# Layer two's input projections as seven block products in place of eight (Strassen's scheme)

## The chip, the cores and the metric

The kernel runs on one core of one Trainium2 chip. A core has five engines with an instruction stream each: PE (TensorE, matrix products into PSUM), DVE (VectorE), ACT (ScalarE), POOL (GpSimd) and SP (SyncE, which here issues nearly all DMAs). They work side by side and wait for each other by semaphores; 16 DMA engines move data between DRAM and the on-chip memory, SBUF. PE adds products up in PSUM, eight banks of 128 partitions x 512 fp32 values; DVE and ACT read PSUM, POOL cannot.

The metric is the device time of one execution in microseconds (us), as a median of several.

## The reference, cut to what matters

Two layers over 1024 tokens (a grid of 16 rows x 64 columns) and 256 context tokens, 1024 features. Layer one is attention with grouped keys; layer two, where the change is, attends within a window of 8 x 16 grid places and to the context:

```python
hx = rms_norm(x, norm_g[i]) * (1.0 + sc_x) + sh_x          # x: 1024 tokens x 1024 features
hc = rms_norm(ctx, norm_g[i]) * (1.0 + sc_c) + sh_c        # ctx: 256 tokens
px = hx @ w_in                                             # w_in: 1024 x 4096, columns q | k | v | z
pkv = hc @ w_in[:, B_WIDTH:3 * B_WIDTH]                    # the context's k and v
...                                                        # attention of 16 heads of 64, with a bias by position
yx = (o * jax.nn.silu(z)) @ w_out
x = x + g_x * yx
return rms_norm(x, final_norm_g)
```

The product `hx @ w_in`, 1024 x 1024 by 1024 x 4096, is the one that is changed.

## The kernel before, in words

**Precision.** PE multiplies fp16 numbers. Each fp32 operand is split into a high and a low fp16 part, and each product is three matmuls: high x high, high x low, low x high, added up in PSUM. Weights are scaled by WS = 32 before they are split. So every operand that reaches PE costs a cast (high) and a subtraction (low) first.

**Tiles.** Tokens come in eight tiles of 128 (t = 0 to 7) and two of context (8, 9). Features are eight chunks of 128 (KT = 8). Heads go in pairs, u = 0 to 7: a pair has 128 columns each of q, k, v and z (the gate).

**Layer two, pair by pair.** `b_load(u)` (L1339) loads the pair's weights, eight blocks of 128 x 512, through a staging tile; `load_w` (L664) splits them with one ACT cast (L670) and one DVE operation (L671) per block. `b_qk(u)` (L1347, matmuls L1360) projects q and k with the weights as stationary operand and 512 tokens as moving one, 24 matmuls to a bank; `b_vz(u)` (L1382, L1393 and, for the context, L1396) projects v and z with a token tile as stationary operand and the 256 weight columns of v and z as moving one. Both use the two PSUM banks called pj in turn, and DVE and ACT take each finished bank out: L1374 to L1379 for q and k, L1403 to L1409 for v and the gate. `b_att(u)` (L1412) computes scores (L1424, L1425), adds the bias on DVE (L1444), takes maxima (L1451), exponentiates on ACT (L1462 to L1465), splits the probabilities (L1042 on DVE or L1045 on POOL), transposes them by DMA, multiplies by v (L1473, L1475) and scales the output (L1491). `o_out` (L1055) splits and transposes it into the tile `ob`. Two tiles of ob are of tag Y0 and the rest of tag Y1.

**The order.** Generators yield after each piece of work, and `timeline` (L478) merges them by written virtual times: pair u's attention from u to u + 1, beside it the projections of pair u + 1 (`b_proj`, L1503) and, from u + 0.5, the weight load of pair u + 2. A `Planner` (L47) then sets the final order on each engine: it simulates the program with a cost for each instruction, works out by when each result is due, and reorders by that. In it, POOL's additions and DVE's operations on two SBUF operands shut each other out (`lock`, L148). Pair 0's projections run before any attention of layer two.

**From layer one to layer two.** `a_out(t)` (L1254, matmuls L1275) projects layer one's output for a token tile in two halves of 512 columns, 24 matmuls each; DVE multiplies by the gate vector (L1279) and POOL adds the residual (L1280). `b_ln(t)` normalises the tile through `ln_tile` (L642): a sum of squares on ACT, the reciprocal root on POOL, two DVE passes on each half, an ACT cast and a DVE subtraction, and two DMA transposes (L661) into `hb_hi` and `hb_lo`, which hold all ten tiles for the whole of layer two. L1516 writes the order: tile t's normalisation beside the output projection of later tiles.

```python
    run_all(steps("l0 o4 l1 o5 l2 o6 l3 o7 l4 o80 l5 o90 l6"))
```

Here `l` is `b_ln` of a tile, `o` is `a_out` of a tile (with a second digit, one half of it).

**The end.** `load_wout` (L1215) brings the output weights, in two sets of tiles (tags X0, X1) that the pairs' weights used before: the first half from virtual time 6.05 on, the second from 7.0 on. `b_out(t, tag)` (L1547, matmuls L1566) does the output projection, the residual, the final norm and the store.

## Time and profile before

| | |
|---|---|
| runs | 1361.56 us median of 3 (1360.18 to 1363.06) |
| profiled execution | 1365.58 us, its span 1363.8 us |
| PE busy | 1329.9 us, 13183 matmuls |
| DVE, ACT, POOL busy | 1003.1, 910.2, 664.7 us |
| one pair of layer two (917.76 to 979.85) | 62.09 us: PE 61.98, DVE 45.55, ACT 45.65, POOL 15.77 busy |

The profile is of one execution. Its page gives the busy time of each engine and, in 40 equal slices of the span, each engine's busy share in tenths and the clock granted to PE. The chain of waits is the chain of work that ended last, followed back from the last instruction; each row has a start, a length and what ran or was waited for. The stretches give the busy time of each engine between two moments. The groups list instructions by source line, engine and operands, with a count, busy time, the mean ns of one, and the idle time in front of them with what ended it. In operand names the numbers are left out: `pb<-hb_hi,wb` is a matmul into a bank `pb...`. A line can be a helper's.

### The profile page before, as it was taken

To read this page: it belongs to the slowest core of one execution; us is meant where nothing else is said; L and a number is where in the kernel's file an instruction comes from. 1 tells how busy PE (TensorE), PEld (TensorE's weight loads), DVE (VectorE), ACT (ScalarE), POOL (GpSimd) and SP (SyncE) were. 2 spreads that over 40 slices of the span, in tenths; PEclk is the share of its full clock that TensorE was granted. 3 is DMA by queue.
4 is the path that set the end of the run, shared out by engine and by line. 5 is a ranking of instruction groups with operands and counts; after the bars stand their busy time and mean duration, and the time that the engine had idled before them with its cause. 6 is when DMAs were issued, how large, how long until landed. Compare 5 with 4: busy or idle time off the path is not lost.

```text
span 1363.8 us, 34709 instructions
## 1 busy us (share of the span) xinstructions
PE 1329.9 (98%) x13183; PEld 927.6 (68%) x13183; DVE 1003.1 (74%) x2647; ACT 910.2 (67%) x2186; POOL 664.7 (49%) x855
## 2 busy tenths in 40 slices
PE   9999999999999999999999999999999999999897
PEld 6457777777777777776554486777768686867543
DVE  5788788878788789887276846777776867777743
ACT  3653788888787876878632437777776777786711
POOL 2573787777778775788743201312222222332332
PEclk9999999999999999999999999999999999999999
DMA  9652577878789777847066725666576656677932
GB/s 352 186 162 76 108 145 156 154 161 166 149 152 169 146 150 138 172 145 210 10 171 175 178 80 120 125 132 138 117 153 110 156 96 146 113 159 141 194 101 102
DMA packets 426959, 198.23 MB, mean 145 GB/s; under 512 B 382560, under 2 KB 389664, under 8 KB 426792
## 3 DMA queue, kind: packets, MB, share of 16 engines
q1 hardware_dynamic: 426216, 195.98, 65.3%
q8 instruction: 103, 1.69, 0.5%
q14 instruction: 64, 0.52, 0.1%
q10 hardware_dynamic: 576, 0.03, 0.0%
HBM read 90.51 MB, written 15.22 MB: 78 GB/s over the span
## 4 chain that ended last, share of the span: by engine, by line
PE 68%; DVE 11%; ACT 9%; DMA 5%; POOL 3%; issue 3%; SPq 1%; DVEq 0%; POOLq 0%; ACTq 0%
PE pa L946 11%; PE pb L1360 9%; PE pvz L1393 9%; PE poa L1275 7%; PE pob L1566 6%; PE st L1183 2%; PE st L1184 2%; PE pkv L817 2%; ACT bpf L1464 2%; PE pm L976 2%; PE bpv L1473 1%; PE pv L1052 1%; PE qpv L1104 1%; PE pv L1053 1%; PE pv L1051 1%
## 5 line engine op out<-in xcount | busy, mean ns | idle before, releaser
L1045 POOL TENSOR_TENSOR pl<-pf,ph 128x256 f16<-128x256 f32 x340 | 234.1, 714 | 58.2 <-ACT pf L1170 44.5
L1045 POOL TENSOR_TENSOR bph<-bpf,bph 128x256 f16<-128x256 f32 (+1 forms) x128 | 99.9, 790 | 319.5 <-ACT bpf L1464 256.3
L946 PE MATMUL pa<-wa,x 128*128 128x256 f16 x1536 | 213.4, 272 | 0.1
L1360 PE MATMUL pb<-hb_hi,wb 128*128 128x512 f16 (+1 forms) x640 | 193.3, 358 | 1.4 <-DVE bk L1379 1.0
L1393 PE MATMUL pvz<-wb,hb_hi 128*128 128x256 f16 x1024 | 175.4, 273 | 0.6 <-DVE bk L1379 0.3
L946 PEld LDWEIGHTS <-x 128*128 128x128 f16 x1536 | 143.2, 97 | 35.7 <-issue 1.3
L1168 ACT ACTIVATE ph<-st 128x512 f16<-128x512 f32 x200 | 119.1, 604 | 60.7 <-PE st L1184 50.0
L1360 PEld LDWEIGHTS <-wb 128*128 128x128 f16 x960 | 92.7, 98 | 72.5 <-issue 2.9
L1393 PE MATMUL pvz<-wb,hb_lo 128*128 128x256 f16 x512 | 139.6, 273 | 0.0
L1170 ACT ACTIVATE pf<-st 128x512 f32<-128x512 f32 x200 | 119.3, 609 | 1.7 <-POOL pl L1045 1.6
L977 DVE TENSOR_REDUCE mxp<-pm 128x1 f32<-128x512 f32 x160 | 107.9, 684 | 13.7 <-PE pm L976 12.3
L1045 POOL TENSOR_TENSOR qpp<-qpf,qpp 128x512 f16<-128x512 f32 x84 | 97.9, 1186 | 38.4 <-ACT qpf L1127 32.2
L1360 PE MATMUL pb<-hb_lo,wb 128*128 128x512 f16 (+1 forms) x320 | 114.4, 358 | 0.0
L1393 PEld LDWEIGHTS <-hb_hi 128*128 128x128 f16 x1024 | 97.1, 98 | 24.2 <-DVE bk L1379 1.1
L1051 PE MATMUL pv<-v,ph 128*128 128x65 f16 x800 | 104.0, 193 | 0.2 <-ACT ph L1168 0.2
L1052 PE MATMUL pv<-v,ph 128*128 128x64 f16 x800 | 104.0, 195 | 0.0
L1053 PE MATMUL pv<-v,pl 128*128 128x65 f16 x800 | 101.4, 192 | 0.5 <-POOL pl L1045 0.5
L1566 PE MATMUL pob<-wob,ob 128*128 128x512 f16 x384 | 86.7, 379 | 2.6 <-DVE bmx L1444 0.9
L1051 PEld LDWEIGHTS <-ph 128*128 128x128 f16 x800 | 75.8, 97 | 19.0 <-ACT ph L1168 0.7
L1462 ACT ACTIVATE bph<-bpf,bnx 128x384 f16<-128x384 f32 (+1 forms) x128 | 68.7, 582 | 27.2 <-DVE bnx L1454 27.1
L1052 PEld LDWEIGHTS <-ph 128*128 128x128 f16 x800 | 75.5, 97 | 12.6
L1053 PEld LDWEIGHTS <-pl 128*128 128x128 f16 x800 | 76.1, 99 | 10.5 <-POOL pl L1045 1.6
(272 smaller groups left out, 3812.1 us busy)
## 6 DMA issues: line engine op xcount, KB each, us to landing
wg<-in_w_mod SPq DMA_DIRECT2D x64, 256.0 KB
wsb<-in_b_in SPq DMA_DIRECT2D x64, 256.0 KB
wm<-in_w_mod SPq DMA_DIRECT2D x16, 512.0 KB
wsa<-in_a_qz SPq DMA_DIRECT2D x32, 256.0 KB
xstage<-in_x SPq DMA_DIRECT2D x8, 512.0 KB
wsoa<-in_a_w_out SPq DMA_DIRECT2D x16, 256.0 KB
x<-in_x SPq DMA_DIRECT2D x8, 512.0 KB
x_d<-x SPq DMA_DIRECT2D x8, 512.0 KB
```

The lines of the kernel that those rows point to most:

```text
L946: T.matmul(ps[:, :, i, :], hA(a, kt, t), wt[w][:, kt, :], start=n == 0, stop=n == 3 * KT - 1)
L977: V.tensor_reduce(mxs[i][:, t, ch:ch + 1], pm, axis=AX.X, op=ALU.max)
L1045: G.tensor_tensor(lo[:, c], p32[:, c], hi[:, c], op=ALU.subtract)
L1051: T.matmul(pv[:, t, :], hi[:, c], v[:, 0:65], start=first and t == 0, stop=False)
L1052: T.matmul(pv[:, t, 0:HD], hi[:, c], v[:, 65:129], start=False, stop=False)
L1053: T.matmul(pv[:, t, :], lo[:, c], v[:, 0:65], start=False, stop=last and t == n - 1)
L1168: S.activation(ph, st, AF.Exp)
L1170: S.activation(p32, st, AF.Exp)
L1275: T.matmul(ps, lhs(a, kt), w[b][:, kt, :], start=n == 0, stop=n == 3 * KT - 1)
L1360: T.matmul(ps[:, 0:n].rearrange("p (t q) -> p t q", q=P), wt[a][:, kt, which * P:(which + 1) * P], hb[b][:, c0 // P:(c0 + n) // P, kt], st ...
L1393: T.matmul(ps[:, :, j, :], hb[a][:, t, kt], wt[w][:, kt, 256:512], start=m == 0, stop=m == 3 * KT - 1)
L1566: T.matmul(ps, ob[kt][:, t // 4, a, c], wout["b"][hf][b][:, kt, :], start=n == 0, stop=n == 3 * KT - 1)
```

## The change

The product is cut into two halves each way: token tiles 0 to 3 and 4 to 7 (A1., A2.), features 0 to 511 and 512 to 1023, and, among a pair's columns, k against q in one group (g = 0) and v against z in the other (g = 1). A 2 x 2 block product has eight block products; the scheme used (Strassen's, in Winograd's form) has seven, of sums of blocks:

- **Token side.** Stored for the whole layer: A11 and A12 (`top`, tiles 0 to 3), S3 = A11 - A21 and S1 = A21 + A22 (`s31`), S2 = S1 - A11 and S4 = A12 - S2 (`s24`), and A22 (`a22`). `b_ln` of tiles 4 to 7 makes them, on DVE, from the tile and the tile four before it; `b_s24` and `b_a22` split, cast and transpose the rest. The context tiles get a tile of their own. `s24`, `a22` and the context lie in the X tags, which layer one's output weights hold until then.
- **Weight side.** `b_load(u, g)` loads four blocks of 128 x 512 for each group. DVE scales the block; ACT and DVE split three of its four sub-blocks as they are; four sums (in fp32) are made, cast and split on POOL (for pair 0 on DVE and ACT). A block has 7 x 128 columns in each part, where it had 4 x 128.
- **Products.** `b_grp` runs products 1, 2, 6, 5, 7, 3, 4, each of 12 matmuls of 512 columns (g = 0) or 48 of 128 columns (g = 1). Products 1, 6, 7, 4 add up in one bank, 5 and 3 in another, 2 in a third allocation. Between them ACT copies the running sum out to SBUF (`keep`, three times a group) and DVE adds a bank to such a copy (three times a group). q, k, v and z are then taken from these sums in SBUF, and the last from PSUM. `cx` does the context's k or v with as many matmuls as before.
- **Memory.** Layer two's outputs `ob` of pairs 0 to 5 go to DRAM (`ob_d`) and return at virtual time 7.18 into the tiles of `top` and `s31`; all of `ob` is of tag Y0. The output weights become 16 tiles, four of which can be loaded before the last pair's projections end; the others take the place of `s24` and `a22`. The transposed probabilities have 7 buffers for 8.
- **Layer one's end.** `a_out` multiplies in place in PSUM and adds the residual on DVE; tiles 4 to 9 have two buffers for the residual stream. The written order becomes the one in the diff.
- **Planner.** DMA costs go by bytes, and fp16 transfers count half.

```diff
-PFB, PHB, PTB = 5, 5, 8
+PFB, PHB, PTB = 5, 5, 7
...
-            d[u] = y_tile((P, 2, 2, 512), F16, f"{kind}{u}", int(kind == "ob" and u > 1))
+            d[u] = y_tile((P, 2, 2, 512), F16, f"{kind}{u}", 0)
...
-            tm = op.tile([P, 512], F32, name=f"tm{t}{hf}", tag="tm", bufs=2)
-            V.tensor_tensor(tm, ps, gts["t"][:, hc], op=ALU.mult)
-            G.tensor_tensor(x1[:, hc], x1[:, hc], tm, op=ALU.add)
+            V.tensor_tensor(ps, ps, gts["t"][:, hc], op=ALU.mult)
+            V.tensor_tensor(x1[:, hc], ps, x1[:, hc], op=ALU.add)
...
+        if t < 4 or t >= NX:
+            for a, r in enumerate(halves(xt, D, nm)):
+                DM.dma_start_transpose(top[a][:, t] if t < NX else late["cx"][:, t - NX, a], r)
+        else:
+            lo, hi = slice(0, 512), slice(512, D)
+            x0, r = x1s[t - 4], lnp.tile([P, 2, 512], F16, name=f"a22r{t}", tag="a22r", bufs=4)
+            a22r[t - 4] = r
+            S.copy(r[:, 0], xt[:, hi])
+            V.tensor_tensor(r[:, 1], xt[:, hi], r[:, 0], op=ALU.subtract)
+            V.tensor_tensor(xt[:, hi], xt[:, lo], xt[:, hi], op=ALU.add)
+            V.tensor_tensor(xt[:, lo], x0[:, lo], xt[:, lo], op=ALU.subtract)
+            V.tensor_tensor(x0[:, lo], xt[:, hi], x0[:, lo], op=ALU.subtract)
+            V.tensor_tensor(x0[:, hi], x0[:, hi], x0[:, lo], op=ALU.subtract)
+            for a, r in enumerate(halves(xt, D, nm)):
+                DM.dma_start_transpose(s31[a][:, t - 4], r)
...
+    def b_load(u, g):
...
+            DM.dma_start(st.rearrange("p a b -> p (a b)"), b_in[u, g, kt])
+            V.tensor_scalar_mul(st, st, WS)
+            w = bq.tile([P, 2, 7, P], F16, name=f"w{nm}", tag="wb", bufs=8)
+            S.copy(w[:, 0, 0:3], st[:, 0:3])
+            V.tensor_tensor(w[:, 1, 0:3], st[:, 0:3], w[:, 0, 0:3], op=ALU.subtract)
+            ts = bq.tile([P, 4, P], F32, name=f"ts{nm}", tag="ts", bufs=2)
+            E = G if u else V
+            E.tensor_tensor(ts[:, 0], st[:, 3], st[:, 0], op=ALU.subtract)
+            E.tensor_tensor(ts[:, 2], st[:, 2], st[:, 3], op=ALU.subtract)
+            E.tensor_tensor(ts[:, 1], st[:, 2], ts[:, 0], op=ALU.subtract)
+            E.tensor_tensor(ts[:, 3], st[:, 1], ts[:, 1], op=ALU.subtract)
+            if u:
+                G.tensor_copy(w[:, 0, 3:7], ts)
+            else:
+                S.copy(w[:, 0, 3:7], ts)
+            E.tensor_tensor(w[:, 1, 3:7], ts, w[:, 0, 3:7], op=ALU.subtract)
...
+        x_ = bank("x")
+        yield from prod(x_, 1, True)
+        e1 = keep(x_, 1)
+        z_ = bank("z")
+        yield from prod(z_, 2, True)
+        V.tensor_tensor(e1, z_, e1, op=ALU.add)
+        done(0, 0, e1)
+        yield from prod(x_, 6, False)
+        e2 = keep(x_, 2)
+        y_ = bank("y")
+        yield from prod(y_, 5, True)
+        e5 = keep(y_, 5)
+        yield from prod(x_, 7, False)
+        V.tensor_tensor(e5, x_, e5, op=ALU.add)
+        done(1, 4, e5)
+        yield from prod(y_, 3, False)
+        V.tensor_tensor(e2, y_, e2, op=ALU.add)
+        done(1, 0, e2)
+        yield from prod(x_, 4, False)
+        done(0, 4, x_)
+        yield from cx(w)
...
+                        if hf == 1 and u in BSPILL:
+                            DM.dma_start(ob_d[u], ob[u].rearrange("p a b c -> p (a b c)"))
...
-    run_all(steps("l0 o4 l1 o5 l2 o6 l3 o7 l4 o80 l5 o90 l6"))
-    items = [(steps("o81 o91 l7 l8 l9"), 0, 0.8, 5120 * 3 + 450 * 6), (b_load(0), 0.05, 0.6, 8),
-             (b_qk(0), 0.85, 1.8, 23040)]
+    for g in range(2):
+        run_all(b_load(0, g))
+    run_all(steps("l0 l1 o4 l2 o5 l3 l4 o6 l5 o7 l6 o80 l7 o90 x0"))
+    run_all(steps("o81 o91 x1"))
+    side[0] = bq
+    items = [(steps("s0 s1 s2 s3 a0 a1 a2 a3 l8 l9"), 0, 0.1, 3400), (b_qk(0), 0.1, 1.0, C_G)]
...
+            items.append((b_qk(u + 1), u, u + 0.48, C_G))
+            items.append((b_vz(u + 1), u + 0.49, u + 0.97 + 0.2 * l_, C_G))
...
+    items.append((load_wob(0, range(0, 4)), 6.5, 6.9, 4))
+    for j in range(3):
+        items.append((once(lambda j=j: ob_back(j)), 7.18 + 0.001 * j, 7.2, 1))
+    items.append((load_wob(0, range(4, 8)), 7.19, 7.21, 4))
+    items.append((load_wob(1, range(0, 8)), 7.2, 7.3, 8))
```

More of the change, by code (lines that the diff above doesn't have):

```diff
@@ L1297, in trunk_kernel, with x_tiles @@
     bpool = ctx.enter_context(tc.tile_pool(name="bpool", bufs=1))
[L1298 to L1299 removed]
+    top = [bpool.tile([P, 4, KT, P], F16, name=f"top{a}", tag=f"top{a}") for a in range(2)]
+    s31 = [bpool.tile([P, 4, KT, P], F16, name=f"s31{a}", tag=f"s31{a}") for a in range(2)]
+    late = {}
+    def x_tiles(j, nm, shape):
+        return [main.tile(list(shape), F16, name=f"{nm}{a}", tag=f"X{j}{a}") for a in range(2)]
     tc.swap_default_side()
@@ L1303, in trunk_kernel, with halves @@
     tc.swap_default_side()
-    def b_ln(t):
-        yield from ln_tile(lnp, x1s[t], 0 if t < NX else 1, hb_hi[:, t], hb_lo[:, t], f"b{t}")
+    def halves(src, w, nm):
+        r = [lnp.tile([P, D], F16, name=f"r{a}{nm}", tag=f"r{a}", bufs=3) for a in range(2)]
+        for hf in range(w // 512):
+            c = slice(hf * 512, hf * 512 + 512)
+            S.copy(r[0][:, c], src[:, c])
+            V.tensor_tensor(r[1][:, c], src[:, c], r[0][:, c], op=ALU.subtract)
+        return r
+    a22r = {}
@@ L1380, in b_qk, with cx @@
                                            op1=ALU.subtract)
+        def cx(w):
+            ps = ps_pj(f"pb{u}c", shape=(P, 2, P))
+            n = 0
+            for kh in range(2):
+                for kt in range(KT // 2):
+                    for a, b in ((0, 0), (0, 1), (1, 0)):
+                        T.matmul(ps, w[kt][:, a, kh], late["cx"][:, :, b, 4 * kh + kt], start=n == 0, stop=n == 23)
+                        n += 1
+                    yield 320
+            done(0, NX, ps, 256)
```

248 lines of the change are left out of this document (152 added, 96 removed).

## The prediction

> **What bounds the kernel now.** I read the page's head first, then the chain of waits, the stretches, and last the groups by line.
>
> ```profile
> span 1363.8 us, 34709 instructions
> PE 1329.9 (98%) x13183; PEld 927.6 (68%) x13183; DVE 1003.1 (74%) x2647; ACT 910.2 (67%) x2186; POOL 664.7 (49%) x855
> PEclk9999999999999999999999999999999999999999
> ```
>
> TensorE (PE) is busy for 98% of the span at a granted clock that never drops. A busy PE need not be a PE at its peak, so the chain of waits is needed (start, length, what). It also prices the matmuls, since runs of one line stand in it without gaps.
>
> ```profile
> 766.15 23.34 PE pb L1360 x120
> 790.04 21.07 PE pvz L1393 x192
> 811.11 2.68 PE pvz L1396 x48
> 814.11 2.59 PE pb L1360 x12
> ...
> 917.76 2.62 PE pb L1360 x24
> ...
> 979.85 2.62 PE pb L1360 x24
> ...
> 1041.94 2.62 PE pb L1360 x24
> ...
> 1304.08 51.81 PE pob L1566 x240
> ```
>
> A 512-column matmul takes 2.59/12 = 0.216 us, a 256-column one 21.07/192 = 0.110, a 128-column one 2.68/48 = 0.056, each with its own weight load. The same event returns every 62.09 us: that is one head pair of layer two. PE's projections there cost 23.34 + 21.07 + 2.68 = 47.1 of it, attention the other 15.0. The stretches (length, then busy time of each engine) show what runs beside PE: between the layers, in one pair, at the end, and in layer one.
>
> ```profile
> core 0: us, PE busy (x) PEld busy (x) DVE busy (x) ACT busy (x) POOL busy (x), PEclk, DMA share, GB/s
> 692.00:766.00 74.00, 74.00 (x345) 33.54 (x344) 53.85 (x79) 23.51 (x43) 30.64 (x27) 1.00 0.77 200
> 766.00:814.00 48.00, 48.00 (x369) 33.84 (x368) 28.16 (x55) 17.61 (x38) 5.93 (x8) 1.00 0.40 98
> 917.76:979.85 62.09, 61.98 (x578) 45.92 (x577) 45.55 (x136) 45.65 (x134) 15.77 (x22) 1.00 0.64 130
> 1250.00:1304.00 54.00, 49.85 (x420) 30.08 (x417) 40.62 (x120) 37.73 (x114) 18.38 (x20) 1.00 0.76 161
> 100.00:665.00 565.00, 552.52 (x6902) 416.85 (x6901) 459.75 (x1242) 433.60 (x894) 411.13 (x525) 1.00 0.71 145
> ```
>
> A pair is bound by PE alone: VectorE (DVE) and ScalarE (ACT) have 16 us to spare, GpSimd (POOL) 46. The question is whether that room holds what the change puts there.
>
> **The matmuls removed.** For q and k, 96 matmuls of 512 columns become 7 x 12 = 84: -12 x 0.216 = -2.6 us. For v and the gate, 192 of 256 columns become 7 x 48 = 336 of 128: 336 x 0.056 = 18.8 for 21.07, -2.3 us. The context's matmuls stay. That is -4.9 us a pair, -39 us over eight: a pair needs 62.09 - 4.9 = 57.2 us of PE. This is the only gain.
>
> The 128-column price is what the change hangs on most directly. The Trainium skill (TensorE: Matmul & The Clock Gate, Back-to-back issue gap) gives 81 ns for a sustained 128-column matmul with its weight load, and 56 ns only for an isolated one. By 81 ns the v products would take 27.2 us and lose 6 instead of gaining 2.3. Here 48 in a row, each with its load, ran at 56 ns, so the trace disagrees and 56 stands.
>
> **What each pair gains elsewhere.** The groups by line over two pairs (917.76 to 1041.94; count, then busy time and mean ns of one), an answer for each engine:
>
> ```profile
> L671 DVE SCALAR_TENSOR_TENSOR wb<-wsb,wb 128x512 f16<-128x512 f32 x16 | 10.9, 683 | 0.2
> L1042 DVE TENSOR_TENSOR bph<-bpf,bph 128x640 f16<-128x640 f32 x12 | 9.9, 821 | 4.4 <-ACT bpf L1465 4.3
> L1491 DVE SCALAR_TENSOR_TENSOR bog<-boc,bse,bsz 128x64 f32<-128x64 f32 x32 | 9.5, 350 | 0.0
> L1404 DVE TENSOR_TENSOR bv<-pvz,bv 128x128 f16<-128x128 f32 x21 | 6.0, 287 | 4.1 <-ACT bv L1403 3.9
> L1375 DVE SCALAR_TENSOR_TENSOR bq<-pb,bq 64x512 f16<-64x512 f32 x8 | 5.5, 685 | 1.3 <-ACT bq L1374 1.2
> L1409 DVE SCALAR_TENSOR_TENSOR bsz<-bth,pvz 128x256 f32<-128x256 f32 x8 | 3.3, 414 | 0.0
> L670 ACT ACTIVATE wb<-wsb 128x512 f16<-128x512 f32 x16 | 9.3, 639 | 0.0
> L1374 ACT ACTIVATE bq<-pb 64x512 f16<-64x512 f32 x8 | 4.7, 594 | 4.5 <-PE pb L1360 2.4 <-DVE bq L1375 2.0
> L1333 POOL TENSOR_TENSOR tb<-tb,mq 128x128 f32<-128x128 f32 x4 | 1.8, 452 | 16.0 <-DMA tb<-tabd 16.0
> ```
>
> And over the whole run:
>
> ```profile
> L800 DVE TENSOR_SCALAR xstage<-xstage,rs_ln 128x1024 f32<-128x1024 f32 x8 | 7.3, 926 | 2.8 <-POOL rs_ln L637 2.8
> L1045 POOL TENSOR_TENSOR qpp<-qpf,qpp 128x512 f16<-128x512 f32 x84 | 97.9, 1186 | 38.4 <-ACT qpf L1127 32.2 <-PE st L1184 2.0 <-PE pmg L610 1.1
> L812 POOL CAST xc_hi<-tf 128x256 f16<-128x256 f32 x8 | 4.0, 494 | 0.5 <-ACT tf L809 0.5
> L671 DVE SCALAR_TENSOR_TENSOR wa<-wsa,wa 128x512 f16<-128x512 f32 x32 | 24.2, 761 | 0.0
> L1042 DVE TENSOR_TENSOR pl<-pf,ph 128x512 f16<-128x512 f32 x30 | 26.3, 878 | 22.2 <-ACT pf L1170 22.0
> L1061 DVE TENSOR_TENSOR ol<-og,ol 128x512 f16<-128x512 f32 x14 | 13.0, 926 | 1.7 <-ACT ol L1060 1.7
> ```
>
> DVE loses eight weight splits (8 x 0.68), ten v remainders (10 x 0.29) and four gate products (4 x 0.41): -10.0. It gains eight scalings (half of L800's 0.93, 0.46; bounds 0 and 0.93), eight splits of 384 columns (between 0.41 at 256 and 0.68 at 512: 0.55), six block sums out of PSUM (0.69 each, as L1375), v remainders in two wide pieces and a narrow one (1.8) and two gate products (1.4): +15.4. Net +5.4, or 5.0 for the overlap of its five more instructions: 50.6 us.
>
> ACT gains six copies out of PSUM (0.59 each) and loses small casts and a quarter of the weight casts: about 47 us. POOL gains, for each of eight blocks, four 128-column sums (0.45), a 512-column cast (twice 0.494 at most, the same at least; 0.75) and a 512-column difference (1.19), 3.7 us: 15.8 + 29.8 = 45 us.
>
> **The shared port.** DVE and POOL don't run independently. The timeline shows it:
>
> ```profile
> 688.67 1.27 POOL L1280 TENSOR_TENSOR x<-x,tm 128x512 f32<-128x512 f32 x1 [2.47 <-DVE tm L1279]
> 715.79 1.65 POOL L1280 TENSOR_TENSOR x<-x,tm 128x512 f32<-128x512 f32 x1 [2.13 <-DVE tm L1279]
> ...
> 697.63 1.28 DVE L657 TENSOR_TENSOR x<-x,lrow 128x512 f32<-128x512 f32 x2
> 715.63 2.36 DVE L657 TENSOR_TENSOR x<-x,lrow 128x512 f32<-128x512 f32 x2
> ```
>
> Two DVE additions take 1.28 us; with a POOL addition begun between them they take 2.36, and POOL's own goes from 1.27 to 1.65. One waits for nearly all of the other. Operations out of PSUM (L1375, L1409) keep their length. The Trainium skill (SBUF — State Buffer, Who interferes with whom) has this as an exclusive lock, for DVE instructions with two SBUF inputs; the rows agree.
>
> The pair would come to 55 DVE instructions of the kind that waits (8 scalings, 8 weight splits, 8 probability splits, 16 output scalings, 4 copies, 2 output splits; and 9 q, k, v and gate operations that now read a sum in SBUF), with POOL busy for 45/57 = 79% instead of 25%. Layer one has POOL at 411/565 = 73%: there L671 takes 0.08 more than in the pairs, L1042's 512-column form 0.19 and L1061 0.24 more than 0.69. At 0.14 that is 55 x 0.14 = 7.7 us, so DVE needs 50.6 + 7.7 = 58.3 us (bounds 55 and 64, at 0.08 and 0.24). PE needs 57.2.
>
> Two engines that need the whole time can't both be full. With DVE at 81% layer one left PE idle for 2.2%; I double that, 57.2 x 1.045 = 59.8 (bounds: 57.6, everything hidden, and 64). Seven pairs run beside attention: 7 x (59.8 - 62.1) = **-16 us**. Pair 0's projections have PE to themselves: **-4.9 us**. Each product must leave its bank within the next product (2.6 us), half of the time that a bank had before; copies of 0.6 us fit while the queues are short.
>
> **Between the layers.** Today DVE has 20 us to spare between 692 and 766, and PE goes from output projections into L1360 without a gap.
>
> ```profile
> L659 DVE TENSOR_TENSOR l16b<-x,h16b 128x512 f16<-128x512 f32 x20 | 19.2, 976 | 0.9 <-ACT h16b L658 0.7
> L1279 DVE TENSOR_TENSOR tm<-poa,gt 128x512 f32<-128x512 f32 x16 | 11.0, 687 | 6.3 <-PE poa L1275 6.2
> L661 SPq DMA_TRANSPOSE hb_hi<-h16b x10: 1232/1234/2075, 699.6 to 778.6; - x10
> ```
>
> DVE gains 15 residual additions from POOL (10 us), five more passes on each of four tiles (13.6), two passes for each of four sums (5.4), and in pair 0's weights 8 x (0.46 + 0.55 + 4 x 0.29 + 0.69) = 22.9 for 5.5. It gets back POOL's blocking (20 x 0.29 on L659, 3 on others). Together about +38 on the 82 us that it works in 692 to 814: 120 us in 117. The third product, at 766 + 5.2 = 771, needs all eight token tiles and four sums; these also wait for layer one's weight tiles, free after half-outputs 8 and 9 (48 x 0.216 = 10.4 before 766, so 756), and for SP to issue eight transposes at 1.23 us: 766 to 768, then their landing. So DVE and the transposes are both just late: **+8 us** (bounds 0 and 16). Behind it waits only PE's next product.
>
> **At the end.** Today the last pair's projections end near 1250; PE then works 49.85 of 54 us. Twelve instead of eight blocks of output weights load behind them (4 x 0.68 us more on DVE, 4 x 0.64 on ACT), and six parked outputs of 512 KB return: 4 MB more. At the stretch's 161 GB/s that is 25 us, at 200 GB/s 20, four of the six early because the first block's tiles come free at the second product. DMA engines have 24% of 54 us left, 13 us: **+4 us** (bounds 0 and 12). The writes of the parked outputs, 0.5 MB a pair beside 130 GB/s x 62 us = 8 MB, I put at nothing: DMA engines are at 64%; without that room it is 0.5 MB/130 GB/s = 4 us a pair. One transpose buffer fewer: nothing, as at most four blocks wait at a time.
>
> **Sum.** -16 - 4.9 + 8 + 4 = -9. The profiled execution took 1365.58 (span 1363.8 and 1.8 around it), 4.0 above the runs' median of 1361.56. 1365.6 - 9 = 1356.6; on the median's scale 1352.6, **1352 us**, own range 1342 to 1358. Chance 0.40.
>
> **Rivals.**
>
> 1. Everything hides, PE stays the only bound. For it: PE is at 99.8% in a pair today. Against it: DVE's 58.3. Pairs of 57.6 (-31.5), -4.9, +3 and +2: -31, 1330 us. Chance 0.22.
> 2. Slower: the port makes DVE the bound. The place is a pair of layer two, POOL's 45 us of weight sums against 55 waiting DVE instructions; at L1061's 0.24 DVE needs 64 us: 7 x 1.9 - 4.9 + 8 = +16, 1378 us. It decides from a pair of 62.1 + (4.9 - 12)/7 = 61.1 us on. Against it: layer one's mean is lower. Chance 0.21.
> 3. The change doesn't do what it says: PE's 39 us turn into waits, pairs at 60.5 (-11), boundary 10, end 8, -4.9: +2, within a few us of 1362. Chance 0.15.
> 4. Slower by PE's own pace: the weight load, not the matmul, sets the step of the 128-column products. One load takes 98 ns where it stands alone:
>
> ```profile
> L1393 PEld LDWEIGHTS <-hb_hi 128*128 128x128 f16 x1024 | 97.1, 98 | 24.2 <-DVE bk L1379 1.1
> ```
>
> At that pace (336 x 0.042 - 4.9) x 8 + 12 = +86, 1447 us. Against it: the 48 in a row. Chance 0.02. The Trainium skill's 81 ns (the page and section above) would make it (336 x 0.025 - 4.9) x 8 + 12 = +40, an estimate by that page, 1402 us.
>
> **How the numbers follow.** About 0.2% is what a measurement of this kernel tells from no change. Faster: 0.40 + 0.22 + 0.02 of rival 3 = 0.64; same 0.11, slower 0.02 + 0.21 + 0.02 = 0.25. The range runs from a little below rival 1 to inside rival 2: 1327 to 1374.
>
> **What would show it.** The products' runs in the chain: 12 in 2.6 us, 48 in 2.7. The period of a pair: 57.6, 59.8, or over 61. DVE busy in a pair: near 100% if I am right, under 90% if rival 1 is; mean of L1042's 640-column form (0.82 today) and of the output scalings (0.35) rising if the port decides. PE's first gap after 766, with DVE or a transpose as its releaser. The time from the last v product to the first output matmul. A PE busy time that falls by much less than 39 us would make the whole prediction wrong.

## The result and the profile after

The changed kernel takes 1377.41 us (median of 4 runs, 1375.47 to 1380.28); the kernel before took 1362.31 us beside it (4 runs, 1360.18 to 1363.91). The ratio is 1.0114, 95% interval 1.0088 to 1.0139: slower by about 15 us, and 3.4 us above the upper end of the range. The profiled executions, 1375.9 and 1365.58 us, differ by 10.3 us; the account below is of these. (A second profiled execution of the changed kernel, r1 below, took 1378.27 us.)

The page of the changed kernel, its head and the shares of its chain of waits:

```profile
span 1374.1 us, 37399 instructions
PE 1305.6 (95%) x14239; PEld 926.8 (67%) x14239; DVE 1143.8 (83%) x2775; ACT 933.7 (68%) x2182; POOL 897.5 (65%) x1171
PE 48%; DVE 27%; ACT 7%; DMA 7%; issue 6%; POOL 5%; SPq 0%; ACTq 0%; DVEq 0%; POOLq 0%
```

PE is busy for 24.3 us less, where 39 were forecast, and waits for more than it saved. The products themselves have the predicted length; the chain shows 48 matmuls of 128 columns and 12 of 512:

```profile
869.61 2.68 PE pv1y L1433 x48
...
1015.81 2.59 PE pb4y L1435 x12
```

The stretches of the changed kernel, columns as before: the gap-free output projections up to the first products, the boundary, three pairs, and the last pair's attention with the first output projections.

```profile
692.00:778.90 86.90, 86.90 (x458) 41.29 (x455) 83.67 (x174) 34.55 (x65) 13.06 (x12) 1.00 0.69 184
778.90:821.10 42.20, 36.57 (x426) 27.46 (x423) 33.26 (x55) 16.22 (x31) 21.13 (x31) 0.96 0.67 147
...
879.20:939.50 60.30, 57.58 (x711) 44.80 (x709) 59.64 (x138) 46.93 (x132) 50.80 (x67) 1.00 0.73 142
939.50:1003.07 63.57, 59.15 (x711) 45.90 (x709) 61.11 (x142) 47.25 (x131) 54.05 (x72) 0.97 0.71 129
1003.07:1067.59 64.52, 59.21 (x710) 46.17 (x709) 62.31 (x146) 48.85 (x135) 51.27 (x70) 0.97 0.68 139
...
1258.26:1316.30 58.04, 49.60 (x381) 28.13 (x381) 40.29 (x121) 39.20 (x117) 19.82 (x22) 1.00 0.96 221
```

In the second of these pairs DVE is busy for 61.11 of 63.57 us (45.55 of 62.09 before) and POOL for 54.05, and PE idles 4.4 us. That DVE sets the pace now is what the experiments have to show.

Cut at the last matmul of layer one's attention and of each pair's projections, the two profiled spans differ like this (all read from the matmuls' starts and ends in the trace):

| us | before | after | difference | predicted |
|---|---|---|---|---|
| start to the end of layer one's attention | 690.0 | 694.4 | +4.4 | 0 |
| from there to the end of pair 0's projections | 123.8 | 126.7 | +2.9 | +8 - 4.9 = +3.1 |
| seven pairs' projections, mean of one | 62.91 | 62.45 | 7 x -0.46 = -3.2 | -16 |
| from there to the end | 109.6 | 115.8 | +6.2 | +4 |

Two rows are near the forecast. The pairs and layer one hold nearly all of the miss, and the experiments are mostly about these.

The mean of the pairs hides something. One by one, from the first to the seventh, they took 60.2, 62.1, 62.1, 62.1, 62.4, 62.1 and 69.4 us before, and 58.2, 60.3, 63.6, 64.5, 62.3, 63.0 and 65.4 after. The first two and the last gained 7.8 us; the four between them, the steady state, lost 4.6.

**The pairs.** DVE's groups by line over two pairs of the changed kernel (count, busy time and mean ns of one, idle time before):

```profile
L1611 DVE SCALAR_TENSOR_TENSOR bog<-boc,bse,bsz 128x64 f32<-128x64 f32 x33 | 14.6, 466 | 0.0
L1389 DVE TENSOR_SCALAR wsb<-wsb 128x512 f32<-128x512 f32 x18 | 12.2, 683 | 0.1
L1392 DVE TENSOR_TENSOR wb<-wsb,wb 128x384 f16<-128x384 f32 x16 | 11.3, 720 | 0.0
L1022 DVE TENSOR_TENSOR bph<-bpf,bph 128x640 f16<-128x640 f32 x12 | 10.6, 885 | 1.2 <-ACT bpf L1585 1.1
...
L1574 DVE TENSOR_SCALAR bnx<-bnx 128x2 f32<-128x2 f32 x16 | 6.6, 412 | 0.1
...
L1457 DVE TENSOR_TENSOR e<-pb4x,e 128x512 f32<-128x512 f32 x1 | 0.7, 673 | 0.0
```

The output scaling went from 350 to 466 ns, a 384-column split takes more than a 512-column one did (683), and an operation on two numbers takes 412 ns (164 before). The sum out of PSUM takes 0.67 us, about the forecast's 0.69. PE's waits in the pairs (what for, us, times, longest):

```profile
PE bsn L1544 <- DVE bmx L1564: 4.4, 7, 1.5
PE pv4x L1433 <- DVE bk L1488: 3.5, 1, 3.5
PE pv3x L1433 <- DVE bk L1488: 3.3, 1, 3.3
```

The longest come in four of the seven pairs (3.1 to 3.5 us), where group 0 hands its bank over to group 1: the first v product waits for DVE to take k out of it. Such a gap can cost more than its length. PE's timeline behind one:

```profile
973.37 0.34 PE L1433 MATMUL pv3x<-wb,top 128*128 128x128 f16 x3 [3.31 <-DVE bk L1488]
...
974.56 1.91 PE L1433 MATMUL pv3x<-wb,top 128*128 128x128 f16 x16
...
976.82 1.88 PE L1433 MATMUL pv3x<-wb,top 128*128 128x128 f16 x29
```

Behind the gap of 3.31 us 16 matmuls take 1.91 us, 119 ns each; from 976.8 on 29 take 1.88, 65 each (attention's matmuls run between them in both). The record of the granted clock has 0.5 for 3.4 us from 973.6 on, and likewise at 789, 1038, 1165 and 1226 us, and twice in layer one (55 and 277 us); before the change it has that only in the last 4 us of the span. At half pace 3.4 us are 1.7 us lost on top of the gap, 12 us for all seven.

Not every gap has this price. The gap of 3.06 us that ends at 1101 (pair 5) has full clock behind it, and one of 1.94 us that ends at 1225 has the slow stretch. In the second execution of the same kernel (r1) it is the other way round: pair 5's gap is followed by 6.8 us at half clock, and the one at 1226 by none. The clock is the last column but two; pair 5 in the first execution and in r1:

```profile
1098.00:1108.00 10.00, 6.13 (x95) 5.43 (x92) 9.65 (x23) 7.30 (x20) 7.92 (x11) 1.00 0.57 129
1096.00:1106.00 10.00, 6.83 (x70) 6.17 (x68) 8.78 (x20) 6.58 (x18) 7.92 (x11) 0.66 0.56 125
```

The Trainium skill (TensorE: Matmul & The Clock Gate, The HAM clock gate) states that the array runs at half its clock after an idle window of about 3.4 us, until it has been busy for about as long, and that these windows run freely. The trace agrees with the length; the gaps that were enough here, 1.9 to 3.6 us, are mostly shorter than that window.

### The profile page after: what moved, and what is told of

Same layout as the page of the kernel before. It is cut to its first block, busy times and chain, and to the rows that moved or that the text cites. A ratio compares the mean times of both kernels' runs of the same rounds, so it can differ in the third digit from the quotient of the medians.

```text
span 1374.1 us, 37399 instructions
## 1 busy us (share of the span) xinstructions
PE 1305.6 (95%) x14239; PEld 926.8 (67%) x14239; DVE 1143.8 (83%) x2775; ACT 933.7 (68%) x2182; POOL 897.5 (65%) x1171
## 4 chain that ended last, share of the span: by engine, by line
PE 48%; DVE 27%; ACT 7%; DMA 7%; issue 6%; POOL 5%; SPq 0%; ACTq 0%; DVEq 0%; POOLq 0%
PE pa L926 11%; PE pob L1734 5%; DMA qpt<-qpp 2%; PE st L1163 2%; PE st L1164 2%; PE pm L956 2%; DVE bpf L1564 2%; PE pkv L797 2%; DVE bog L1611 2%; PE qpv L1084 2%; DVE bk L1488 1%; PE pv L1032 1%; DVE bph L1022 1%; DVE mxp L957 1%; PE pv L1033 1%
## 5 line engine op out<-in xcount | busy, mean ns | idle before, releaser
L1025 POOL TENSOR_TENSOR bph<-bpf,bph 128x256 f16<-128x256 f32 (+1 forms) x128 | 111.6, 882 | 102.5 <-ACT bpf L1584 72.6
L1435 PEld LDWEIGHTS <-wb 128*128 128x128 f16 x672 | 63.9, 98 | 73.1 <-issue 9.7
L1433 PEld LDWEIGHTS <-s 128*128 128x128 f16 x1536 | 88.5, 98 | 1.9
L1163 PE MATMUL st<-q,k 128*128 128x512 f16 x200 | 76.0, 380 | 2.2 <-ACT pf L1150 2.0
L1164 PE MATMUL st<-q,k 65*128 65x512 f16 x200 | 75.5, 382 | 1.9 <-DMA q<-zt 1.9
L1584 ACT ACTIVATE bpf<-bpf,bnx 128x384 f32<-128x384 f32 (+1 forms) x128 | 74.3, 581 | 0.0
L1403 POOL TENSOR_TENSOR wb<-tsb,wb 128x512 f16<-128x512 f32 x56 | 71.6, 1289 | 0.5
L1099 DVE CUSTOM_DVE_ANT_0 qpf<-qs,zero 128x512 f32<-128x512 f32 x96 | 65.4, 683 | 7.0 <-PE qs L1097 4.3
```

Of the source, the lines that this page charges most:

```text
L1025: G.tensor_tensor(lo[:, c], p32[:, c], hi[:, c], op=ALU.subtract)
L1163: T.matmul(so, k1[:, g, kc], q1[:, :, i, :], start=True, stop=False)
L1164: T.matmul(so, k2[0:65, g, kc], q2[0:65, :, i, :], start=False, stop=True)
L1433: T.matmul(ps[:, t], a_blk(a, kt, m)[:, t], w[kt][:, b, WIX[m]], start=f, stop=l, skip_group_check=not first)
L1584: S.activation(pf[:, 0:n], pf[:, 0:n], AF.Exp, bias=m, accum_out=sums[:, t % 4, 0:1])
```

## The experiments

Each ratio is to the kernel before, timed on the same chip.

### What the port costs in the pairs

**x1** leaves the weight sums of pairs 1 to 7 out:

```diff
+            if u:
+                wb[u, g].append(w)
+                yield 1.0
+                continue
             ts = bq.tile([P, 4, P], F32, name=f"ts{nm}", tag="ts", bufs=2)
```

> Leaves out a part of the computation: for pairs 1 to 7 the four weight sums of each block, their cast and their difference (all of POOL's share of the weight load); the four products that need them use plain sub-blocks in their place, so PE, DVE and ACT issue what they did. Theory (the shared port: POOL's 30 us of weight sums a pair hold up DVE): DVE in a pair falls from 61 to 51-53 us, its output scalings from 466 to about 340 ns and its weight scalings from 683 to 420; PE becomes the bound again, pairs of 58 to 59 us for 63, total 1377 - 7 x 4.5 = about 1346 (1340 to 1352). Rival (DVE's own added instructions, or the hand-over of the two banks, hold PE): pairs stay at 61 or more, total over 1363.

1354.31 us, 0.9928 (0.9902 to 0.9954), 2 us above the expected range; pairs of 59.19. Pairs 2 to 5 of the changed kernel and of x1, and x1's DVE groups over two pairs:

```profile
879.25:1129.88 250.63, 233.63 (x2834) 181.61 (x2833) 243.89 (x555) 189.13 (x525) 211.09 (x282) 0.99 0.70 136
881.60:1115.50 233.90, 229.32 (x2834) 178.92 (x2832) 202.66 (x556) 189.65 (x527) 65.05 (x88) 1.00 0.76 147
```

```profile
L1392 DVE TENSOR_TENSOR wb<-wsb,wb 128x384 f16<-128x384 f32 x16 | 9.4, 588 | 0.4 <-ACT wb L1391 0.4
L1615 DVE SCALAR_TENSOR_TENSOR bog<-boc,bse,bsz 128x64 f32<-128x64 f32 x33 | 8.5, 304 | 0.0
L1389 DVE TENSOR_SCALAR wsb<-wsb 128x512 f32<-128x512 f32 x16 | 6.8, 454 | 1.5 <-DMA wsb<-in_b_in 1.5
```

The same DVE instructions (555 and 556 of them) are busy for 243.89/4 = 61.0 us a pair with POOL's sums and for 202.66/4 = 50.7 without, where the prediction had 50.6 before it added the port. POOL's work costs DVE 10.3 us a pair. PE's clock is never slowed in x1's pairs.

**p1** puts POOL's added work, and nothing else, into the kernel before, its results into a tile that nobody reads:

```diff
+                G.tensor_tensor(ts[:, 0], st[:, 3], st[:, 0], op=ALU.subtract)
+                ...                       # the four sums, as in the change
+                G.tensor_copy(w[:, 0], ts)
+                G.tensor_tensor(w[:, 1], ts, w[:, 0], op=ALU.subtract)
```

> The kernel before with POOL's added work alone: for pairs 1 to 7 POOL makes the four sums, the cast and the difference of each block from the staged weights into scratch tiles that nobody reads; PE, DVE and ACT issue what they did before. It measures the disputed cost by itself: how much longer DVE's instructions get. Theory (the port: POOL held for 45 to 50 us of a pair): DVE's busy time in a pair rises from 45.5 to 54-58 us with the same instructions, output scalings from 350 to 430-500 ns, the weight splits on DVE from 683 to 750-850, while instructions out of PSUM (685 and 553 ns) keep their length; the pair stays near 62 to 63 because PE's 62 still sets it; ratio 1.000 to 1.012. Rival (POOL and DVE share without loss; the changed kernel's DVE is full of its own new instructions): DVE busy stays under 49, rows unchanged.

1374.5 us, 1.0078 (1.0061 to 1.0095); its pairs take 64.3 us for 62.9. Pairs 2 to 5, and the DVE groups over 124 us of them:

```profile
874.30:1130.30 256.00, 249.01 (x2308) 183.18 (x2306) 213.70 (x539) 185.21 (x537) 198.89 (x284) 1.00 0.64 127
```

```profile
L671 DVE SCALAR_TENSOR_TENSOR wb<-wsb,wb 128x512 f16<-128x512 f32 x16 | 13.9, 876 | 0.2 <-ACT wb L670 0.2
L1500 DVE SCALAR_TENSOR_TENSOR bog<-boc,bse,bsz 128x64 f32<-128x64 f32 x29 | 13.5, 497 | 0.0
...
L1042 DVE TENSOR_TENSOR bph<-bpf,bph 128x640 f16<-128x640 f32 x12 | 13.1, 1093 | 2.3 <-ACT bpf L1474 2.2
L1388 DVE SCALAR_TENSOR_TENSOR bk<-pb,bk 64x512 f16<-64x512 f32 x8 | 5.5, 688 | 1.6 <-ACT bk L1387 1.4
```

POOL's load alone makes the three groups between SBUF tiles 28 to 42% longer (683, 350 and 821 before) and leaves the one out of PSUM at 688. It costs 10 us although DVE, at 83%, is not full. Two sizes were not as expected: DVE is busy for 213.70/4 = 53.4 us a pair (45.55 before), a little less than the 54 to 58 of the theory, and the pair is longer than the 62 to 63 expected.

**x2** takes eight scalings a pair from DVE (the weights stay unscaled):

```diff
-            V.tensor_scalar_mul(st, st, WS)
+            if not u:
+                V.tensor_scalar_mul(st, st, WS)
```

> Leaves out a part of the computation: DVE's scaling of the weights by 32 in pairs 1 to 7 (8 instructions a pair, 683 ns each as they ran, 5.5 us of DVE). POOL's work is untouched. If DVE is what a pair waits for, whatever fills it, 5 us less on DVE shorten the pair by 3 to 5 us until PE's 57.4 is met: pairs of 59 to 60, total 1350 to 1357. If POOL's own chain of weight sums, or the hand-over of a bank at the end of each group, set the pace, pairs stay within 1 us of 63 and the total over 1370.

1369.42 us, 1.0025 (1.0005 to 1.0044); pairs of 60.59. About 5.5 us of DVE work are gone from a pair, and 1.9 us of its time, which is neither of the two lengths expected. Two groups and a stretch show why:

```profile
L1612 DVE SCALAR_TENSOR_TENSOR bog<-boc,bse,bsz 128x64 f32<-128x64 f32 x34 | 16.4, 504 | 0.1
L1393 DVE TENSOR_TENSOR wb<-wsb,wb 128x384 f16<-128x384 f32 x16 | 13.4, 856 | 0.0
```

```profile
939.00:1065.00 126.00, 120.95 (x1477) 95.97 (x1476) 121.76 (x274) 98.69 (x272) 101.65 (x143) 0.97 0.70 143
```

What is left waits longer (466 and 720 ns in the changed kernel), and DVE is as full as it was. In this run, work taken from DVE is largely given back to the port as long as POOL's work stays.

**y1** moves work instead of leaving it out: ACT scales and casts in one pass, DVE scales and subtracts in one, and POOL keeps the four sums only.

```diff
-            V.tensor_scalar_mul(st, st, WS)
-            S.copy(w[:, 0, 0:3], st[:, 0:3])
-            V.tensor_tensor(w[:, 1, 0:3], st[:, 0:3], w[:, 0, 0:3], op=ALU.subtract)
+            S.activation(w[:, 0, 0:3], st[:, 0:3], AF.Copy, scale=WS)
+            V.scalar_tensor_tensor(w[:, 1, 0:3], st[:, 0:3], WS, w[:, 0, 0:3], op0=ALU.mult, op1=ALU.subtract)
...
-            if u:
-                G.tensor_copy(w[:, 0, 3:7], ts)
-            else:
-                S.copy(w[:, 0, 3:7], ts)
-            E.tensor_tensor(w[:, 1, 3:7], ts, w[:, 0, 3:7], op=ALU.subtract)
+            S.activation(w[:, 0, 3:7], ts, AF.Copy, scale=WS)
+            V.scalar_tensor_tensor(w[:, 1, 3:7], ts, WS, w[:, 0, 3:7], op0=ALU.mult, op1=ALU.subtract)
```

> Moves work off the shared port without leaving any out: ACT makes both high parts of a weight block with the factor 32 in the cast (5 us more a pair on ACT), DVE makes both low parts with the factor in the operation (its 8 scalings of 0.42 us a pair go, 8 differences of 512 columns at 0.69 come: +2 us), POOL keeps the four sums alone (its 8 casts and 8 differences go, 0.83 and 1.28 each as they ran: -17 us of 54). Theory (what the port is held for sets the pair): the port's work falls by about 12 us, pairs of 60.0 to 61.0 for 62.45, total some 10 to 17 us under the changed kernel's 1.0114 of the kernel before: ratio 0.999 to 1.004. Rival (DVE's own volume sets it): 2 us more on DVE a pair, ratio over 1.015.

1355.6 us, 0.9922 (0.9899 to 0.9946); pairs of 59.82.

```profile
939.00:1065.00 126.00, 121.27 (x1472) 92.99 (x1470) 119.76 (x296) 109.72 (x298) 71.18 (x111) 1.00 0.74 144
```

POOL falls from 85 and 79% to 56%, ACT takes up 87%, DVE stays at 95%. The gain is larger than expected (ratio 0.999 to 1.004, pairs of 60 to 61). That the pair comes to the forecast's 59.8 us is chance, as the work is split differently. The change's arithmetic pays once enough of POOL's work is off the port.

**z2** is z1 (below) with more of the probabilities' splits on POOL: DVE keeps every third tile instead of every second.

```diff
-BEV, BLAG = 2, 4
+BEV, BLAG = 3, 4
```

> z1 with every third instead of every second probability split on DVE, the rest on POOL, which has 40% idle in y1's pairs: 2.7 splits a pair leave DVE (2.2 us) for POOL (4 us more of the port). Theory (DVE is what y1's pairs of 59.8 wait for, and the port is no longer full): pairs of 58.5 to 59.3, ratio 0.002 to 0.006 under z1's. Rival (time on the port counts, whichever engine holds it): pairs of 60 or more, no gain.

1353.37 us, 0.9926 (0.9908 to 0.9944), pairs of 59.71 for z1's 59.69: no gain, and short of the rival's 60. DVE lost work and POOL gained it (86.89 busy in 126 us for 77.64). The total is above z1's because layer one ends 6.4 us later (698.5 for 692.1).

### The hand-over of the bank

**y2** copies the last product out on ACT before k is split, so that the bank is free after one operation instead of after k's casts and remainders:

```diff
-        done(0, 4, x_)
+        done(0, 4, x_ if g else keep(x_, 4))
```

> Changes the hand-over alone: the last sum of the q and k group is copied out of its bank by one ACT instruction, as the three before it, and k is made from the copy; the bank is free after 0.6 us instead of after two ACT and two DVE instructions in turn. Theory (four gaps of 3.1 to 3.5 us before the v group in pairs 3 to 6, each with a slow clock of 3.41 us behind it that costs 1.7 more, come from those DVE instructions): the gaps shrink under 1 us and the slow stretches go: 4 x (2.5 + 1.7) = 10 to 17 us less, ratio 0.999 to 1.005. Rival (the port and DVE are full anyway; what PE does not wait for here it waits for a little later): within 4 us, ratio 1.008 to 1.015, with new waits on the scores (bsn) in place of the gaps.

1380.25 us, 1.0111 (1.0086 to 1.0136); pairs of 61.87. The waits for the hand-over are gone, and others are in most of their place:

```profile
PE bsn L1544 <- DVE bmx L1564: 5.5, 4, 3.6
PE bsc L1544 <- ACT bpf L1585: 2.2, 3, 1.4
PE pv1x L1433 <- POOL tsb L1395: 2.0, 1, 2.0
```

The pairs gained 4 us together, for 10 to 17 expected, so the bank was mostly where DVE's lateness showed, not its cause. The total does not show these 4 us, because layer one ends later (698.7 for 694.4) and the boundary and the end are longer (128.9 and 120.0 for 126.7 and 115.8).

### Between the layers

**x4** gives pair 0's sums to POOL, and **y3** issues half of the `s24` transposes from ACT's queue:

```diff
-            E = G if u else V
+            E = G
```

> Moves pair 0's weight sums and differences from DVE to POOL, which worked only 13 us of the 87 between 692 and 779, while DVE worked 83.7. The result is unchanged. Theory (the gap between the layers comes from DVE's queue: it has no idle time from 740 to 790): about 15 us of DVE work go; the last sums of tokens are ready some 8 us earlier and PE's waits of 1.2 and 3.6 us before product 6 vanish with the slow clock behind them: total 5 to 8 us less, 1369 to 1372. Rival (SP's transposes and the tiles that layer one's output weights hold until 768 set that time): within 2 us of 1377. Second rival (the port): POOL's sums hold DVE up for as long as they relieve it: 1377 or more.

```diff
-            DM.dma_start_transpose(late["s24"][a][:, t], r)
+            (S if a else DM).dma_start_transpose(late["s24"][a][:, t], r)
```

> Changes the stage between the layers alone: four of the eight last transposes (the low parts of the four token sums) are issued by ACT, which worked 35 of the 87 us there, instead of SP. Theory (SP issues eight transposes at 1.28 us in a row behind the last sum, and PE waits 1.2 and 3.6 us for them): they are issued 5 us earlier, both waits and the slow clock behind them go, 5 to 6 us from the end of layer one's attention to the end of pair 0's projections (126.7 us): 121 to 122, and the ratio is 1.004 to 1.010 but for what another plan does to layer one. Rival (the last sums themselves are late, on DVE, or the DMA engines are busy): 126 to 128 us.

x4: 1374.8 us, 1.0074 (1.0053 to 1.0095); the stretch from layer one's end to pair 0's takes 129.3 us (126.7 with the change). Its stretch up to the first products, and PE's waits behind it:

```profile
688.00:774.00 86.00, 86.00 (x458) 41.30 (x455) 80.47 (x132) 34.70 (x64) 46.75 (x57) 1.00 0.67 188
PE pb0x L1435 <- DMA s<-r0s: 3.5, 1, 3.5
PE pb0x L1435 <- DMA s<-r1s: 3.1, 1, 3.1
```

DVE was hardly relieved: it has 42 instructions fewer (132 for 174), but is busy for 80.47 us for 83.67, with POOL at 46.75 for 13.06. The port, the second rival, fits that. The last six transposes start no earlier, 86.1 us behind layer one's end for 84.3, and then follow each other on SP's queue as in the changed kernel. The clock is at half for 10.2 us there, from 780.3 on, for 3.4 in the changed kernel. So x4 does not tell DVE's part from the transposes'; PE waits for transposes that are themselves issued behind DVE's late sums.

y3: 1395.09 us, 1.0217 (1.0196 to 1.0238), the stretch 145.7 us. Its transposes of `s24` by queue (count, ns of an issue, first and last start), the waits of SP's queue from 770 to 806 us, and three of each kind on SP alone in the changed kernel (start, length):

```profile
L1337 SPq DMA_TRANSPOSE s<-r0s x4: 1231/1250/1281, 772.0 to 790.0; - x4
L1337 ACTq DMA_TRANSPOSE s<-r1s x4: 1248/1248/1507, 775.6 to 799.6; - x4
SPq L1337 <- DMA s<-r1s: 6.5, 1, 6.5
SPq L1342 <- DMA s<-r1s: 5.0, 1, 5.0
```

```profile
778.69 4.62 SPq L1337 DMA_TRANSPOSE s<-r0s  x3
783.40 4.07 SPq L1337 DMA_TRANSPOSE s<-r1s  x3
```

On one queue these six start 1.3 to 2.0 us apart. On two, (799.6 - 772.0)/7 = 3.9 us pass on average from one of the eight to the next (1.9 in the changed kernel), and once all sums are ready a transpose behind one of the other queue starts 3.1 to 3.3 us after it. The trace puts the waits of SP's queue down to the landing of ACT's transposes. The Trainium skill (DMA: Bandwidth & Descriptors, Latency and other measured facts) states that transposes on two queues must not be in flight at once and that software has to put them in sequence; the trace agrees, as they take turns.

**z1** is y1 with a buffer of its own for the scratch of the squares, which shared three buffers with tiles that wait for their transposes:

```diff
-        sq = lnp.tile([P, D], F16, name="lsq" + nm, tag="r0", bufs=3)
+        sq = lnp.tile([P, D], F16, name="lsq" + nm, tag="lsq", bufs=1)
```

> The version with casts on ACT and differences on DVE (y1, ratio 0.992), and one more change: the scratch of the sum of squares between the layers has a buffer of its own; so far it takes one of the three of r0, which are free only when a transpose has landed (ACT sat 4.5 us in front of a square for that, and tile 7's square came at 760). Theory (the chain of the last token tile starts late for want of these buffers): from the end of layer one's attention to the end of pair 0's projections 118 to 123 us for y1's 125.6 and the changed kernel's 126.7; ratio 0.987 to 0.991 but for the plan of layer one. Rival (DVE's full queue and SP's eight transposes in a row set that time whatever the square does): 124 to 128 us, ratio within 0.003 of y1's.

1350.99 us, 0.9915 (0.9889 to 0.9942). The stretch takes 123.9 us, y1's 125.6 (118 to 123 were expected); as a time it can't be told from y1's 0.9922.

### The end

**y4** leaves the return of the parked outputs out; the outputs of pairs 6 and 7 are used in their place.

```diff
-    for j in range(3):
-        items.append((once(lambda j=j: ob_back(j)), 7.18 + 0.001 * j, 7.2, 1))
```

> Leaves out a part of the computation: the parked outputs of pairs 0 to 5 are not read back, and the output projection uses those of pairs 6 and 7 in their place; 3 MB less move behind the last pair. Theory (the end is 6 us longer than before because DMA engines, 96% busy from 1258 to 1316, bring transposed probabilities late): from the end of the last projections to the end of the span 110 to 112 us for 115.8. Rival (it is the output weights, twelve blocks for eight on ACT and DVE behind the last pair): 114 or more.

1387.66 us, 1.0167 (1.0139 to 1.0196); the end takes 122.2 us, longer than with the return; 3.4 us of it are lost in two stretches at half clock, at 1270 and 1277 us. So the return is not shown to cost anything, and the run doesn't clear it either, since the order on all engines came out different. In the changed kernel PE's waits behind 1258 us are for DVE first:

```profile
PE bsn L1544 <- DVE bmx L1564: 4.5, 5, 1.3
PE pob L1734 <- DVE wobh L1660: 1.9, 2, 1.1
```

What makes the end 6 us longer stays open.

### Layer one

The change leaves the code of layer one's attention as it is but for what the planner thinks a DMA costs. **x3** takes that edit back:

```diff
-            by = 2 if outs[0].dtype == F16 else 4
-            ro = min(min(run) * by, 4096)
-            return (470.0 if len(list(outs[0].ap)) < 3 else 600.0), m * by / ro * (11 + ro * 0.0432) / 16
+            ro = min(min(run), 1024) * 4
+            return (470.0 if len(list(outs[0].ap)) < 3 else 600.0), m * 4 / ro * (11 + ro * 0.0432) / 16
```

> Undoes one part of the change: the planner's DMA costs are those of the kernel before (an fp16 transfer counted as fp32). Layer one's last attention matmul came 4.4 us later in the changed kernel (694.4 for 690.0), though nothing but this cost touches layer one's plan. Theory: the changed plan of layer one is the cause: the 4.4 us come back, total 1373 (1370 to 1375). Rival: it is noise of a plan, or of the whole program's due times: total within 2 us of 1377.

1374.37 us, 1.0064 (1.0044 to 1.0084), layer one's end at 686.4. By itself that settled nothing: x4, with the new cost, ends at 688.1, and the other variants with the new cost lie between 692.1 and 699.7. So the changed kernel was profiled once more, unchanged:

> The changed kernel, unchanged, profiled a second time. In the first profile layer one's attention ends at 694.4 us, 4.4 later than in the kernel before, though its code there is the same; in the other variants it ends anywhere from 686.4 to 699.7. Theory (the place of the instructions, set by the planner for the whole program, makes the difference): the second profile gives 694.4 within 1.5 us, and the other stages agree with the first profile as closely: boundary 126.7, seven pairs 62.45 on average, tail 115.8. Rival (one execution differs from the next by that much, and the plan has no part): layer one's end moves by 4 us or more. Ratio to the kernel before as in the first timing, 1.009 to 1.014.

1376.72 us, 1.0086 (1.0054 to 1.0117); layer one's end at 692.4, boundary 126.7, pairs 62.81, end 117.7. An execution moves layer one's end by 2 us, more than the 1.5 expected and less than the variants differ; r1 lacks the two slow stretches in layer one (3.4 us lost), and its end comes 2 us earlier. What the kernels with a late end of layer one share is one wait of PE up to there, for the transposed probabilities. In the kernel before and in the changed one:

```profile
PE qpv L1104 <- DMA qpt<-qpp: 0.6, 1, 0.6
```

```profile
PE qpv L1084 <- DMA qpt<-qpp: 7.5, 9, 2.5
```

It is 0.6 to 1.8 us in the three kernels with the old cost (before, x3, p1; layer one's end at 686.3 to 690.0) and 4.8 to 9.6 us in every one with the new (688.1 to 699.7). **w1** puts the new cost alone into the kernel before (the diff of x3, the other way round):

> The kernel before with the planner's new DMA cost and nothing else. Theory (with fp16 transfers counted at half, the planner puts what needs a transfer too early behind it, and PE waits for transposed probabilities in layer one): waits of PE for qpt of 5 to 8 us up to 690 us, where the kernel before has 0.6; layer one's attention ends 3 to 6 us later, at 693 to 696; ratio 1.002 to 1.005. Rival (the scatter of plans and executions): waits for qpt under 2 us, the end within 2 us of 690.0, ratio within 0.001 of 1.

1372.66 us, 1.0062 (1.0038 to 1.0085); layer one ends at 695.8, and the wait is there:

```profile
PE qpv L1105 <- DMA qpt<-qpp: 6.6, 5, 2.7
```

The effect is larger than was expected of it (0.2 to 0.5%), and its sign and place are the theory's: the other stages take what they took before (124.0 to the end of pair 0, pairs of 62.84, an end of 109.6). Layer one also has two stretches at half clock here, at 415 and 445 us. The order that the planner writes with its new estimates brings PE to `qpt` before the transposes land. **w2** is z1 with the old cost:

> The best variant so far (sums cast on ScalarE, a buffer of its own for the squares; 1350.99 us, layer one's end at 692.1, waits for qpt 7.0) with the planner's DMA cost as before the change. Theory: waits for qpt under 2 us, layer one's end at 686 to 688, and with pairs of 59.7 and a tail of 115 to 118 a time of 1344 to 1349 us, ratio 0.986 to 0.990. Rival (scatter): waits for qpt above 4 us or an end of 690 and later; or, the old cost misplaces the parked outputs' transfers and the tail gives back what layer one gains: tail above 119, ratio 0.991 as before.

1344.65 us (1341.55 to 1348.69), 0.9857 (0.9837 to 0.9877); layer one's end at 686.9, with 0.7 us of waits for `qpt`, the stretch behind it 122.0, pairs of 59.20, the end 116.5.

```profile
span 1339.8 us, 37266 instructions
PE 1296.0 (97%) x14239; PEld 918.7 (69%) x14239; DVE 1107.8 (83%) x2767; ACT 964.0 (72%) x2238; POOL 782.1 (58%) x1059
```

This version beats both kernels: the seven products, the weight split on ACT and DVE, the squares' own buffer, and the planner's costs left alone.

## Why the prediction was wrong, step by step

- **The matmuls removed: right.** 48 in 2.68 and 12 in 2.59 us. In pairs without a slowed clock PE needs 57.6 us (57.58 in the second), and x1's four pairs come to 229.32/4 = 57.3; the sum said 57.2. Rival 4 is out. PE's busy time fell by 24.3 us only, which I had named as a sign that the whole prediction is wrong. It is not that here: some 12 of the 15 us between are matmuls at half clock, busy for longer.
- **What each pair gains elsewhere: right.** DVE takes 50.7 us without POOL's new work (x1), for the predicted 50.6.
- **The shared port: mechanism right, term too small.** 10.3 us on 55 instructions are 0.19 us each, where I took 0.14 from layer one. POOL was busy for 84% of pairs 2 to 5 (211.09 of 250.63), for the 79% that I worked with. I counted no wait for the instructions on few numbers either (412 ns for 164).
- **The pair's length, "I double that": the step that failed.** I took the pair from PE's time, 57.2 us with 4.5% of idle time on top, beside a DVE that needs 58.3, and got 59.8. DVE needed 61.0, more than that whole pair; so DVE sets the length, at 97% busy, and PE is idle or slowed for 5 us of a pair, not 2.6. The pairs took 62.45 on average. With 61.0 in place of 58.3, and DVE as full as I had it, the step would have given 62.6. 12.9 of the 19.3 us of error (+10.3 for -9) are here. On PE the lateness shows as gaps of 3 us at the hand-over and stretches at half clock, which the trace of before could not show: its longest gap is 2.5 us, and its clock stays full behind it.
- **Rival 2** has the mechanism at a weaker price: DVE's bound is 61, not 64. The four middle pairs together did get longer, as it says; the first two and the last kept seven pairs 3.2 us below the old ones. That its 1378 us lies within 1 us of the result is luck: it has +13 for the pairs, and nothing for layer one.
- **Layer one: a term that was missing.** The planner's edit stood in the change and had no line in the sum. It cost 4.4 us in the profile (2.4 in r1), and alone 0.62% (0.38 to 0.85), some 8 us of the kernel before by the medians and 5 by the profiled executions. With x3 at 1.0064 and the change at 1.0114 and 1.0086 (r1), it is a quarter to a half of the slowdown.
- **Between the layers: right in size.** +2.9 for +3.1. I named DVE and the transposes as both just late; PE does wait for transposes there, and no run separates the two.
- **At the end: +6.2 for +4**, within its bounds (+8.1 in r1); the cause that I gave, the return of the parked outputs, was not shown. The parked outputs' writes, put at nothing, were not tested.

## What to carry to other kernels

A matmul saved is worth the idle time of the engines that prepare its operands, and two engines that share a port have less of it than their busy times say: price every instruction between SBUF tiles with the other engine's load on it, and move work to an engine off the port before leaving any out. An edit to a scheduler's costs reaches every stage, so it needs its own term and its own run. Gaps of 2 to 4 us on PE can cost 1.7 us and more again in clock, though not each time, so look for the one wait per period that grows long, and ask which engine is late rather than which buffer. Look at the periods one by one, too: here the first and the last gained and hid that the steady state lost.

## What was not expected of the hardware

- Time freed on DVE was taken by the port: without 5.5 us of work DVE was as full as before, with the same operations at 856 for 720 and 504 for 466 ns (x2).
- The same gap of 3.06 us was followed by a stretch at half clock in one execution of the same kernel and not in the other (r1, the changed kernel); 1.94 us could be enough.
- An operation on 128 x 2 numbers with one SBUF input took 412 ns beside a busy POOL and 163 without (changed kernel, x1). The Trainium skill (SBUF — State Buffer, Who interferes with whom) names `tensor_scalar`, `copy` and `cast` as operations that can take both ports and so contend with GpSimd; the trace agrees.
- Transposes that alternate between two queues start 3.1 us and more apart, on one queue from 1.3 us on, as SP's queue waits for the landing of ACT's (y3).
